# Conv-FFN on one core: seven of twelve units of the first down projection in the seven-product form, parked weight sums every six chunks, and gelu as one ScalarE function

## The chip, the core and the metric

One core of a Trainium2 chip runs one layer of a decoder trunk. TensorE (PE) multiplies, VectorE (DVE) and ScalarE (ACT) prepare operands and evacuate results, GpSimd (POOL) and SyncE (SP) issue most of the DMAs. The metric is the device time of one execution in microseconds (us); the median of several runs is compared.

## What is computed

The layer is an attention mixer and a gated feed-forward block with a short convolution. The change lies in the second:

```python
def conv_ffn(h, w_up, conv_w, conv_b, w_down):
    a, b = jnp.split(h @ w_up, 2, axis=-1)               # h: 256 x 2048, w_up: 2048 x 11264
    ap = jnp.pad(a, ((0, 0), (CONV_WIDTH - 1, 0), (0, 0)))
    c = conv_b
    for j in range(CONV_WIDTH):                          # width 3
        c = c + conv_w[j] * ap[:, j:j + S]
    return (jax.nn.gelu(c, approximate=True) * b) @ w_down   # w_down: 5632 x 2048
...
    h = rms_norm(x, norm_ffn_pre[l])
    y = conv_ffn(h, ffn_w_up[l], ffn_conv_w[l], ffn_conv_b[l], ffn_w_down[l])
    x = x + rms_norm(y, norm_ffn_post[l])
```

All tensors are float32, with 256 tokens, model width 2048 and feed-forward width 5632.

## The kernel before

**Three products for one.** A float32 operand is split into a high and a low part of 128x1024 or 128x512 each. `convert` casts the loaded tile `raw` to `whi` on ScalarE (L163) and subtracts on VectorE (`wlo = raw - whi`, L164). `mm3` (L198 to L200) then multiplies high by high, low by high and high by low. A chunk of weights is one load of 512 KB on SP's queue, one cast, one subtraction and the matmuls that use it. `whi` and `wlo` lie in rings of four buffers: a conversion runs at most some chunks ahead of the matmuls.

**The up part.** Columns of `w_up` are worked in eleven blocks of 512 (c = 0 to 10). A block is 16 chunks, eight for the gate input `a` (accumulators `ua`) and eight for `b` (`ub`). In each chunk of c >= 1 the helper `gemm_cols` runs eight matmuls with the high part, 512 columns wide (L1340), and eight with the low part, 256 wide (L1344); odd chunks take the low part first. After each half `evac` adds two halves of each accumulator into a tile `f` on ScalarE and VectorE (L1361, L1362), and after the block `conv_cols` (L1230 to L1240) does convolution, gelu and gate for four groups of 128 columns: one ScalarE and two VectorE operations for the convolution, then `Square`, a VectorE operation, `Tanh`, a VectorE operation for gelu, then the product with b and a split.

**The first down part.** When c = 5 is done, the 24 finished groups of 128 rows are multiplied with rows 0 to 3071 of `w_down`, in two pairs of column blocks (p = 0, 1, each 1024 columns; `pair_gemm`). A pair is a list of twelve units of two rows of blocks each. A plain unit ("p") is 2 x 4 block products, so 24 matmuls; it converts 2 chunks of 1024 columns. A seven-product unit ("s") replaces the eight block products by seven, 21 matmuls; it needs sums of the activations (`token_sums`, names `sa`, `sm`, `s`) and sums of weight blocks, and converts 3.5 chunks. `PAIR_ORDER` lists the units: six s in each pair before. The four extra accumulators `qd` of the s units lie in the other half of the eight PSUM banks; after the last s unit `end_sums` (L350 to L363) copies and adds them into tiles `ds` (`COPY ds<-qd` on ScalarE, then VectorE adds), which frees those banks for whatever comes next, in pair 1 the accumulators `ua` of block c = 6.

**Parked weight sums.** The sums of weight blocks are made earlier and parked in DRAM (`park_sums`, L235 to L269). One park is: two loads of 512 KB from `w_down` into a staging tile `ta_s` on POOL's queue (L245); two VectorE subtractions and a store of the first half (L257); two more subtractions and a store of the second half (L262). The subtractions are L252, all kept in program order on VectorE. There is a single staging buffer (`STAGE`, tag "sg"), so the loads of a park wait on POOL until the stores of the park before it have landed. `park_a` makes the sums for the first down part; four of them (`EARLY`) are made during the attention, the others in the up part, at steps set by `t0` (a step is one chunk).

**Order.** Each engine runs its own in-order queue. In this region a scheduler decides at build time in which order an engine's instructions stand; at run time an instruction that waits holds up everything behind it on its engine.

Of the kernel before, what the change touches and what calls it, by code (L numbers as in the profile page):

```python
# [37 lines left out]
SC_MLA = (128 + 64) ** -0.5  # L38
GELU_C = math.sqrt(2.0 / math.pi)
GELU_R = math.sqrt(0.044715)  # L40


def trunk_layer(ctx, tc, x, x_cols_in, conv_cols_in, g_mix_post, g_ffn_post, w_in, w_q, w_kv,
# [1116 lines left out]
    def x2_norm(t):  # L1160
        for j in range(4):
            act.activation(jk(f"xj{t}_{j}"), x2[t][j], AF.Square, accum_out=ssh[t][:, j:j + 1])
        v = sb(p3, [P, 1], f"vh{t}")
        vec.tensor_reduce(v, ssh[t], axis=AX.X, op=ALU.add)
        vec.tensor_scalar(v, v, 1.0 / D, EPS, op0=ALU.mult, op1=ALU.add)
        r = rsqrt(v, 1, f"rf{t}", p3)
        r2 = sb(p3, [P, 1], f"rfh{t}")
        vec.tensor_scalar(r2, r, 0.5, None, op0=ALU.mult)
        rf[t] = (r, r2)

# [49 lines left out]
    resid(1)  # L1220
    gT, dsum, dsum_all = [[], []], [], []
    GH, GL = pair_view(gT[0]), pair_view(gT[1])
# [4 lines left out]
    def conv_cols(k, a, b, slot):  # L1227

        w0, w1, w2, cb_ = (cvT[:, 44 * q + k:44 * q + k + 1] for q in range(4))
        cc = sb(p6, [P, 256], f"cc{k}", tag="cc", bufs=3)  # L1230
        uu = sb(p6, [P, 256], f"uu{k}", tag="uu", bufs=3)
        act.activation(cc, a, AF.Identity, scale=w2, bias=cb_)  # L1232
        vec.scalar_tensor_tensor(cc[:, 1:256], a[:, 0:255], w1, cc[:, 1:256], op0=ALU.mult, op1=ALU.add)
        vec.scalar_tensor_tensor(cc[:, 2:256], a[:, 0:254], w0, cc[:, 2:256], op0=ALU.mult, op1=ALU.add)
        act.activation(uu, cc, AF.Square, scale=GELU_R)
        vec.scalar_tensor_tensor(uu, uu, 1.0, cc, op0=ALU.add, op1=ALU.mult)
        act.activation(uu, uu, AF.Tanh, scale=GELU_C)
        vec.scalar_tensor_tensor(uu, uu, 1.0, cc, op0=ALU.add, op1=ALU.mult)
        vec.tensor_tensor(uu, uu, b, op=ALU.mult)  # L1239
        split_to(GH(slot), GL(slot), uu)  # L1240

    def norm_row():
# [3 lines left out]
        for t in range(NT):  # L1246
            vec.tensor_scalar(dg[:, t * P:(t + 1) * P], ident, rf[t][0][:, 0:1], None, op0=ALU.mult)
        pr = pst.tile([P, 512], F32, name="rrow", tag="t")
# [14 lines left out]
    def ffn_up0():  # L1263
# [3 lines left out]
        def evac(acc, q):  # L1267
            f = sb(p6, [P, 1024], f"f{q}_0", tag="f" + "ab"[q], bufs=2)
            for t in range(NT):
                a = f[:, t * 512:(t + 1) * 512]  # L1270
                act.activation(a, acc[t], AF.Copy, scale=rf[t][q][:, 0:1])
                sa[t][q] = a
# [18 lines left out]
        gT[0][:], gT[1][:] = highs(g), lows(g)  # L1291
        dsum_all[:] = [sb(p7, [P, D], f"ds{t}") for t in range(NT)]
        dsum[:] = [[d[:, j * 512:(j + 1) * 512] for j in range(4)] for d in dsum_all]
        norm_row()
# [23 lines left out]
    def sums_tile(name, i):  # L1318
        return sb(*((p3,) if i < 2 else (p6,)), [P, D], f"{name}_{i}", F32R, tag=(f"x2_{i}" if i < 2 else "gp"))

    def x_raws():
        t = sb(p3, [P, D], f"xraw{now[0]}", tag="x2_1")
        more_raw[:] = [raw_of, lambda name: t[:, 0:1024], raw_of, lambda name: t[:, 1024:2048], raw_of, raw_x]

    def g_sums(u):

        if u % 2 == 0:
            s_tiles[u // 2] = sums_tile("s", u // 2)
        hi, lo = (s_tiles[u // 2][:, (u % 2) * 1024 + i * 512:(u % 2) * 1024 + (i + 1) * 512] for i in range(2))
        a, m = (sb(s_pool[0], [P, 512], f"s{n}{u}", tag="hx", bufs=2) for n in "am")  # L1330
# [21 lines left out]
    def ffn_up(c, slot0):  # L1352
# [3 lines left out]
        def evac(acc, q):  # L1356
            f = sb(p6, [P, 1024], f"f{q}_{c}", tag="f" + "ab"[q], bufs=2)
            for i in range(4):
                a = f[:, i * 256:i * 256 + 256]
                sc = (1.0, 0.5)[q]  # L1360
                act.activation(a, acc[i][:, 256:512], AF.Copy, scale=sc)  # L1361
                vec.scalar_tensor_tensor(a, acc[i][:, 0:256], sc, a, op0=ALU.mult, op1=ALU.add)  # L1362
                sa[q].append(a)
# [11 lines left out]
    for i in range(sum(NA) - EARLY):  # L1375
        parked_a.append(park_a(i + EARLY, t0=now[0] + 8 + 15 * i // 2, **STAGE))
    for c in range(1, 6):
# [7 lines left out]
        if c == 5:  # L1385
            at(now[0] + 6, more_raw.clear)
            for u, t in ((2, 8), (3, 11)):
                at(now[0] + t, lambda u=u: g_sums(u))
# [76 lines left out]
    def finish(t, n=4):  # L1465
# [175 lines left out]
```

## Time and profile before

| | |
|---|---|
| median of three runs | 1453.33 us (1453.3 to 1454.87) |
| the profiled execution | 1454.23 us, its span 1452.5 us |
| TensorE clock granted, mean | 0.998 |
| DMA traffic over the span | 359.69 MB, mean 248 GB/s |
| busy in 840 to 860 us (block c = 2) | PE 20.00, VectorE 18.05, ScalarE 12.68 us of 20; DMA share 0.93 |
| busy in 980 to 1000 us (end of c = 5) | PE 20.00, VectorE 12.70, ScalarE 9.95 us of 20; DMA share 0.77 |

The span is the time from the first to the last instruction. A row of a timeline starts with its start and its duration in microseconds, then engine, line, operation, output<-inputs, shape and count; brackets tell how long the engine stood idle before it and what it waited for. Matmuls overlap in the records, so their pitch (from start to start) is what counts, not the duration. In the profiled run block c = 1 of the up part begins at about 772 us, c = 2 at 818.7 us, the two pairs of the first down part fill 997 to 1119 us, and blocks c = 6 to 10 follow.

### The profile page before, as it was taken

The page shows a single profiled execution, that of the slowest core. Times are in us where ns is not written, and L with a number is a line of the kernel's source. Part 1 is how long each engine was busy: PE and PEld are TensorE (multiplying, and loading weights), DVE is VectorE, ACT ScalarE, POOL GpSimd, SP SyncE. Part 2 cuts the span into 40 slices and gives each one's busy share as a digit, 9 for nine tenths or more (in the row PEclk, how much of TensorE's full clock was granted, in tenths as well). Part 3 has the DMA queues.
Part 4 walks back from the last instruction along what each step waited for, and adds up shares of the span by engine and source line. Part 5 has one row for each costly group of instructions (what it writes and reads, how often), then busy time and mean ns, then how long its engine had stood idle before and what let it go on. Part 6 is the DMA issues. An engine that isn't in the chain of part 4 may idle for free.

```text
span 1452.5 us, 21438 instructions
## 1 busy us (share of the span) xinstructions
PE 1442.0 (99%) x7518; PEld 1233.7 (85%) x7518; DVE 1160.4 (80%) x2056; ACT 864.7 (60%) x1422; POOL 118.2 (8%) x222
## 2 busy tenths in 40 slices
PE   9999999999999999999999999999999999999997
PEld 7888888888898888888888888888888888888886
DVE  7788896766878775888789899876777797987798
ACT  7588864544555655546566565655646565555673
POOL 2022110010000001100000111000000101000000
PEclk9999999999999999999999999999999999999999
DMA  8655376699875759965666898866878888789965
GB/s 309 209 171 163 103 261 188 219 327 294 244 220 178 230 164 319 348 232 183 219 205 208 272 331 288 292 206 210 310 276 262 312 276 292 246 265 309 340 219 203
DMA packets 164684, 359.69 MB, mean 248 GB/s; under 512 B 20816, under 2 KB 31952, under 8 KB 164576
## 3 DMA queue, kind: packets, MB, share of 16 engines
q1 hardware_dynamic: 143152, 282.49, 59.8%
q0 software_dynamic: 21280, 75.56, 15.0%
q8 instruction: 59, 0.97, 0.3%
q14 instruction: 49, 0.40, 0.1%
q10 hardware_dynamic: 144, 0.26, 0.1%
HBM read 323.62 MB, written 34.65 MB: 247 GB/s over the span
## 4 chain that ended last, share of the span: by engine, by line
PE 91%; DVE 4%; ACT 2%; DMA 2%; issue 1%; SPq 0%; DVEq 0%; ACTq 0%
PE ub L1340 10%; PE ua L1340 9%; PE accg L200 9%; PE accg L198 9%; PE accg L199 9%; PE ub L1344 5%; PE ua L1344 5%; PE cd L199 2%; PE cd L198 2%; PE cd L200 2%; DVE wlo L164 2%; DMA raw<-in_ffn_w_up_dram 1%; PE cdc L199 1%; PE cdc L198 1%; PE cdc L200 1%
## 5 line engine op out<-in xcount | busy, mean ns | idle before, releaser
L163 ACT CAST whi<-raw 128x1024 fp32r<-128x1024 f32 (+2 forms) x497 | 504.0, 1023 | 373.9 <-PE accg L200 109.1
L164 DVE TENSOR_TENSOR wlo<-raw,whi 128x1024 fp32r<-128x1024 f32 (+2 forms) x497 | 585.0, 1188 | 172.0 <-ACT whi L163 165.6
L198 PE MATMUL accg<-whi,ahl 128*128 128x512 f32 (+1 forms) x416 | 162.5, 391 | 0.0
L200 PE MATMUL accg<-whi,ahl 128*128 128x512 f32 (+1 forms) x416 | 160.7, 386 | 0.0
L199 PE MATMUL accg<-wlo,ahl 128*128 128x512 f32 (+1 forms) x416 | 159.8, 384 | 0.0
L1340 PE MATMUL ub<-ahl,whi 128*128 128x512 f32 x640 | 154.7, 391 | 0.2 <-DVE uu L1239 0.2
L1340 PE MATMUL ua<-ahl,whi 128*128 128x512 f32 x640 | 154.6, 391 | 0.0
L1340 PEld LDWEIGHTS ub<-ahl,whi 128*128 128x128 f32 x640 | 117.5, 188 | 23.1 <-ACT cc L1232 0.5
L1340 PEld LDWEIGHTS ua<-ahl,whi 128*128 128x128 f32 x640 | 117.6, 188 | 22.7
L198 PE MATMUL accg<-whi,bhl 128*128 128x512 f32 x256 | 100.8, 394 | 0.0
L200 PE MATMUL accg<-whi,bhl 128*128 128x512 f32 x256 | 100.0, 391 | 0.0
L199 PE MATMUL accg<-wlo,bhl 128*128 128x512 f32 x256 | 99.9, 390 | 0.0
L200 PEld LDWEIGHTS accg<-whi,ahl 128*128 128x128 f32 x416 | 78.1, 188 | 15.2
L199 PEld LDWEIGHTS accg<-wlo,ahl 128*128 128x128 f32 x416 | 78.3, 188 | 13.0
L198 PEld LDWEIGHTS accg<-whi,ahl 128*128 128x128 f32 x416 | 78.2, 188 | 12.9
L1344 PEld LDWEIGHTS ub<-ahl,wlo 128*128 128x128 f32 x640 | 82.2, 191 | 3.3
L1344 PEld LDWEIGHTS ua<-ahl,wlo 128*128 128x128 f32 x640 | 82.2, 191 | 3.1
L1344 PE MATMUL ua<-ahl,wlo 128*128 128x256 f32 x640 | 83.7, 283 | 0.0
L1344 PE MATMUL ub<-ahl,wlo 128*128 128x256 f32 x640 | 83.3, 283 | 0.0
L200 PEld LDWEIGHTS accg<-whi,bhl 128*128 128x128 f32 x256 | 48.1, 188 | 10.1
L199 PEld LDWEIGHTS accg<-wlo,bhl 128*128 128x128 f32 x256 | 48.1, 188 | 9.6
L198 PEld LDWEIGHTS accg<-whi,bhl 128*128 128x128 f32 x256 | 48.1, 188 | 9.6
(659 smaller groups left out, 2679.7 us busy)
## 6 DMA issues: line engine op xcount, KB each, us to landing
raw<-in_ffn_w_up_dram SPq DMA_DIRECT2D x142, 512.0 KB, 4.9
raw<-in_w_in_dram SPq DMA_DIRECT2D x105, 512.0 KB, 4.6
raw<-in_ffn_w_down_dram SPq DMA_DIRECT2D x66, 512.0 KB, 5.6
xraw<-in_ffn_w_up_dram SPq DMA_DIRECT2D x34, 512.0 KB, 5.2
raw<-in_w_o_swa_dram SPq DMA_DIRECT2D x32, 512.0 KB, 5.3
raw<-in_w_o_mla_dram SPq DMA_DIRECT2D x26, 512.0 KB, 6.9
raw<-in_w_out_dram SPq DMA_DIRECT2D x26, 512.0 KB, 4.6
ta_s<-in_ffn_w_down_dram POOLq DMA_DIRECT2D x24, 512.0 KB, 5.9
```

Source lines behind the costliest of these rows:

```text
L163: act.copy(hi[:, a:b], raw[:, a:b])
L164: vec.tensor_tensor(lo[:, a:b], raw[:, a:b], hi[:, a:b].bitcast(F32), op=ALU.subtract)
L198: pe.matmul(o, ah, bh, start=start, stop=False)
L199: pe.matmul(o, ah, bl, start=False, stop=False)
L200: pe.matmul(o, al, bh, start=False, stop=stop)
L1340: pe.matmul(acc[i], hi[:, c], hn[p][:, j * 512:(j + 1) * 512], start=p + j == 0, stop=stop)
L1344: pe.matmul(acc[i][:, 0:256], lo[:, c], hn[p][:, j * 512:j * 512 + 256], start=False, stop=False)
```

## The change

- `PAIR_ORDER` has seven s units in both pairs instead of six, each in place of a plain unit; the last s unit and the plain unit behind it stay at the end.
- That makes 14 parks instead of 12. Four are still made early; the ten others are made in blocks c = 1 to 4, one every 6 chunks from step 5 on, where there were eight, one every 7.5 chunks from step 8 on.
- The sums of the activations for the seventh unit (u = 6) are made in c = 5. Their tile shares a buffer with the tile `ds0_1`, into which pair 1's `end_sums` copies its first accumulator; the tiles `ds` are now opened where they are first written, one for each token half and pair.
- Gelu is one ScalarE function instead of two ScalarE and two VectorE operations. The factor 0.5 that the old form needed is gone, so `evac` becomes a copy and an add.

```diff
@@ conv_cols
         act.activation(cc, a, AF.Identity, scale=w2, bias=cb_)
...
-        act.activation(uu, cc, AF.Square, scale=GELU_R)
-        vec.scalar_tensor_tensor(uu, uu, 1.0, cc, op0=ALU.add, op1=ALU.mult)
-        act.activation(uu, uu, AF.Tanh, scale=GELU_C)
-        vec.scalar_tensor_tensor(uu, uu, 1.0, cc, op0=ALU.add, op1=ALU.mult)
+        act.activation(uu, cc, AF.Gelu_apprx_tanh)
         vec.tensor_tensor(uu, uu, b, op=ALU.mult)
@@ ffn_up0
-        dsum_all[:] = [sb(p7, [P, D], f"ds{t}") for t in range(NT)]
-        dsum[:] = [[d[:, j * 512:(j + 1) * 512] for j in range(4)] for d in dsum_all]
@@
+    def first_sums_of(p):
+        for t in range(NT):
+            d = sb(s_pool[0], [P, 1024], f"ds{t}_{p}")
+            for j in range(2):
+                dsum[t][2 * p + j] = d[:, j * 512:(j + 1) * 512]
+        return [dsum[t][2 * p + j] for t in range(NT) for j in range(2)]
@@ g_sums
-        if u % 2 == 0:
-            s_tiles[u // 2] = sums_tile("s", u // 2)
-        hi, lo = (s_tiles[u // 2][:, (u % 2) * 1024 + i * 512:(u % 2) * 1024 + (i + 1) * 512] for i in range(2))
+        if u == 6:
+            s = sb(s_pool[0], [P, 1024], f"s{u}", F32R, tag="ds0_1")
+            hi, lo = s[:, 0:512], s[:, 512:1024]
+        else:
...
@@ ffn_up, evac
-                sc = (1.0, 0.5)[q]
-                act.activation(a, acc[i][:, 256:512], AF.Copy, scale=sc)
-                vec.scalar_tensor_tensor(a, acc[i][:, 0:256], sc, a, op0=ALU.mult, op1=ALU.add)
+                act.copy(a, acc[i][:, 256:512])
+                vec.tensor_tensor(a, acc[i][:, 0:256], a, op=ALU.add)
@@
     for i in range(sum(NA) - EARLY):
-        parked_a.append(park_a(i + EARLY, t0=now[0] + 8 + 15 * i // 2, **STAGE))
+        parked_a.append(park_a(i + EARLY, t0=now[0] + 5 + 6 * i, **STAGE))
...
         if c == 5:
             at(now[0] + 6, more_raw.clear)
-            for u, t in ((2, 8), (3, 11)):
+            for u, t in ((6, 4), (2, 8), (3, 11)):
@@
-                      lambda u: s_of[u], p, d, parked=parked_a[NA[0] * p:])
+                      lambda u: s_of[u], p, lambda p=p: first_sums_of(p), parked=parked_a[NA[0] * p:])
@@
-PAIR_ORDER = ("pppspsspsssp", "ppspspsspssp")
+PAIR_ORDER = ("ppsspsspsssp", "ppsspsspsssp")
...
-LINE_Z = 48
+LINE_Z = 64
```

**Where instructions move.** In block c = 2 the rows of VectorE's queue run from the last subtraction of one park to the first of the next (`ta_s` is the staging tile, `wlo` a weight conversion, `f` an evacuation, `cc` the convolution). Before:

```order
L252 TENSOR_TENSOR ta_s<-ta_s 128x512
L164 TENSOR_TENSOR wlo_8733<-raw_8730,whi_8732 128x1024
L164 TENSOR_TENSOR wlo_8757<-xraw_8729,whi_8756 128x1024
L164 TENSOR_TENSOR wlo_8779<-raw_8776,whi_8778 128x1024
L1362 SCALAR_TENSOR_TENSOR f_2_8691<-ua_0_8446,f_2_8691 128x256
L1362 SCALAR_TENSOR_TENSOR f_2_8691<-ua_1_8447,f_2_8691 128x256
L1362 SCALAR_TENSOR_TENSOR f_2_8691<-ua_2_8448,f_2_8691 128x256
L1362 SCALAR_TENSOR_TENSOR f_2_8691<-ua_3_8449,f_2_8691 128x256
L164 TENSOR_TENSOR wlo_8800<-xraw_8729,whi_8799 128x1024
L1233 SCALAR_TENSOR_TENSOR cc_8950<-f_2_8691,cvT,cc_8950 128x255
L164 TENSOR_TENSOR wlo_8822<-raw_8819,whi_8821 128x1024
L1234 SCALAR_TENSOR_TENSOR cc_8950<-f_2_8691,cvT,cc_8950 128x254
```

Five conversions stand here, and a sixth before the next park's first subtraction, seven rows further on. The same place on VectorE of the changed kernel, from the third and last row of subtractions of a park to the next park:

```order
L162 TENSOR_TENSOR wlo_8719<-raw_8716,whi_8718 128x1024
L250 TENSOR_TENSOR ta_s<-ta_s 128x512 x3
L162 TENSOR_TENSOR wlo_8740<-xraw_8715,whi_8739 128x1024
L162 TENSOR_TENSOR wlo_8762<-raw_8759,whi_8761 128x1024
L1363 TENSOR_TENSOR f_2_8674<-ua_0_8438,f_2_8674 128x256
L1363 TENSOR_TENSOR f_2_8674<-ua_1_8439,f_2_8674 128x256
L1363 TENSOR_TENSOR f_2_8674<-ua_2_8440,f_2_8674 128x256
L1363 TENSOR_TENSOR f_2_8674<-ua_3_8441,f_2_8674 128x256
L162 TENSOR_TENSOR wlo_8783<-xraw_8715,whi_8782 128x1024
L1229 SCALAR_TENSOR_TENSOR cc_8933<-f_2_8674,cvT,cc_8933 128x255
L162 TENSOR_TENSOR wlo_8805<-raw_8802,whi_8804 128x1024
L250 TENSOR_TENSOR ta_s<-ta_s 128x512
```

Four conversions stand between the two parks now. Counted over all ten parks of the up part, the distance from the last subtraction of a park to the first of the next is 4, 2, 4, 4, 4, 4, 5, 4 and 4 conversions; before it was 5, 6, 6, 7, 6, 7 and 5.

The second place is the end of pair 1, VectorE's rows of `end_sums` (`qd_3`, `qd_2`, `qd_1` are extra accumulators, `cd_0` a plain one, the last `wlo` rows belong to block c = 6). Before:

```order
L164 TENSOR_TENSOR wlo_11332<-raw_11329,whi_11331 128x1024
L355 TENSOR_TENSOR ds_7772<-ds_7772,qd_3_10887 128x512
L164 TENSOR_TENSOR wlo_11355<-raw_11352,whi_11354 128x1024
L356 TENSOR_TENSOR ds_7773<-ds_7772,qd_2_10886 128x512
L359 TENSOR_TENSOR ds_7773<-ds_7773,qd_1_10885 128x512
L360 TENSOR_TENSOR ds_7772<-ds_7772,qd_1_10885 128x512
L1410 TENSOR_TENSOR ds_7772<-ds_7772,cd_0_10804 128x512
```

And in the changed kernel:

```order
L162 TENSOR_TENSOR wlo_11308<-raw_11305,whi_11307 128x1024
L162 TENSOR_TENSOR wlo_11331<-raw_11328,whi_11330 128x1024
L353 TENSOR_TENSOR ds_1_11240<-ds_1_11240,qd_3_10852 128x512
L162 TENSOR_TENSOR wlo_11358<-raw_11355,whi_11357 128x1024
L354 TENSOR_TENSOR ds_1_11241<-ds_1_11240,qd_2_10851 128x512
L1412 TENSOR_TENSOR ds_1_11240<-ds_1_11240,cd_0_10769 128x512
L357 TENSOR_TENSOR ds_1_11241<-ds_1_11241,qd_1_10850 128x512
L358 TENSOR_TENSOR ds_1_11240<-ds_1_11240,qd_1_10850 128x512
```

The adds stand one conversion of block c = 6 later than before, and the two that free `qd_1` stand behind the add of a plain accumulator. On ScalarE the copy that starts them (`COPY ds<-qd`) stood behind the casts of the pair's last plain unit; in the changed kernel it stands two casts later, here with the last cast of the plain unit, two casts of block c = 6 and the copy:

```order
L161 CAST whi_11265<-raw_11263 128x1024
L161 CAST whi_11307<-raw_11305 128x1024
L161 CAST whi_11330<-raw_11328 128x1024
L352 COPY ds_1_11240<-qd_0_10849 128x512
L161 CAST whi_11357<-raw_11355 128x1024
```

The copy moved behind the casts of the first two chunks of block c = 6. ScalarE's list also has one `ACT_TABLE_LOAD` more, at the first gelu in block c = 1.

More of the change, by code (lines that the diff above doesn't have):

```diff
@@ L38 @@
 SC_MLA = (128 + 64) ** -0.5
-GELU_C = math.sqrt(2.0 / math.pi)
-GELU_R = math.sqrt(0.044715)
 def trunk_layer(ctx, tc, x, x_cols_in, conv_cols_in, g_mix_post, g_ffn_post, w_in, w_q, w_kv,
@@ L1166, in x2_norm @@
         r = rsqrt(v, 1, f"rf{t}", p3)
-        r2 = sb(p3, [P, 1], f"rfh{t}")
-        vec.tensor_scalar(r2, r, 0.5, None, op0=ALU.mult)
-        rf[t] = (r, r2)
+        rf[t] = r
     w_done = [0]
@@ L1220, in trunk_layer @@
     resid(1)
-    gT, dsum, dsum_all = [[], []], [], []
+    gT, dsum = [[], []], [[None] * 4 for t in range(NT)]
     GH, GL = pair_view(gT[0]), pair_view(gT[1])
@@ L1246, in norm_row @@
         for t in range(NT):
-            vec.tensor_scalar(dg[:, t * P:(t + 1) * P], ident, rf[t][0][:, 0:1], None, op0=ALU.mult)
+            vec.tensor_scalar(dg[:, t * P:(t + 1) * P], ident, rf[t][:, 0:1], None, op0=ALU.mult)
         pr = pst.tile([P, 512], F32, name="rrow", tag="t")
@@ L1270, in evac @@
                 a = f[:, t * 512:(t + 1) * 512]
-                act.activation(a, acc[t], AF.Copy, scale=rf[t][q][:, 0:1])
+                act.activation(a, acc[t], AF.Copy, scale=rf[t][:, 0:1])
                 sa[t][q] = a
@@ L1325, in g_sums @@
     def g_sums(u):
-        if u % 2 == 0:
-            s_tiles[u // 2] = sums_tile("s", u // 2)
-        hi, lo = (s_tiles[u // 2][:, (u % 2) * 1024 + i * 512:(u % 2) * 1024 + (i + 1) * 512] for i in range(2))
+        if u == 6:
+            s = sb(s_pool[0], [P, 1024], f"s{u}", F32R, tag="ds0_1")
+            hi, lo = s[:, 0:512], s[:, 512:1024]
+        else:
+            if u % 2 == 0:
+                s_tiles[u // 2] = sums_tile("s", u // 2)
+            hi, lo = (s_tiles[u // 2][:, (u % 2) * 1024 + i * 512:(u % 2) * 1024 + (i + 1) * 512] for i in range(2))
         a, m = (sb(s_pool[0], [P, 512], f"s{n}{u}", tag="hx", bufs=2) for n in "am")
@@ L1405, in trunk_layer, with pair_add @@
     for p in range(2):
-        d = [dsum[t][2 * p + j] for t in range(NT) for j in range(2)]
         c = pair_gemm(f"d{p}", w_down, 0, 1024 * p, PAIR_ORDER[p], lambda k, t: (GH(k)[:, t * P:(t + 1) * P], GL(k)[:, t * P:(t + 1) * P]),
-                      lambda u: s_of[u], p, d, parked=parked_a[NA[0] * p:])
-        for n_, (o, x_) in enumerate(zip(d, c)):
-            at(now[0] + n_, lambda o=o, x_=x_: vec.tensor_tensor(o, o, x_, op=ALU.add))
+                      lambda u: s_of[u], p, lambda p=p: first_sums_of(p), parked=parked_a[NA[0] * p:])
+        def pair_add(i, p, x_):
+            o = dsum[i // 2][2 * p + i % 2]
+            vec.tensor_tensor(o, o, x_, op=ALU.add)
+        for i, x_ in enumerate(c):
+            at(now[0] + i, lambda i=i, p=p, x_=x_: pair_add(i, p, x_))
     more_raw.clear()
@@ L1476, in result @@
             a, b = 512 * j, 512 * j + 512
-            vec.scalar_tensor_tensor(dsum_all[t][:, a:b], dsum_all[t][:, a:b], r[:, 0:1], x2_all[t][:, a:b], op0=ALU.mult, op1=ALU.add)
-            nc.sync.dma_start(out[t * P:(t + 1) * P, a:b], dsum_all[t][:, a:b])
+            vec.scalar_tensor_tensor(dsum[t][j], dsum[t][j], r[:, 0:1], x2_all[t][:, a:b], op0=ALU.mult, op1=ALU.add)
+            nc.sync.dma_start(out[t * P:(t + 1) * P, a:b], dsum[t][j])
         for j in range(n):
```

## Prediction

> **What bounds the kernel now.** I read the page first: the busy times, then the chain that ended last, then TensorE's own waits, then the pitch of its matmuls.
>
> ```profile
> span 1452.5 us, 21438 instructions
> PE 1442.0 (99%) x7518; PEld 1233.7 (85%) x7518; DVE 1160.4 (80%) x2056; ACT 864.7 (60%) x1422; POOL 118.2 (8%) x222
> ...
> PE 91%; DVE 4%; ACT 2%; DMA 2%; issue 1%; SPq 0%; DVEq 0%; ACTq 0%
> ```
>
> TensorE is busy for 99% of the span and makes 91% of the chain. The view of its waits has three rows in all:
>
> ```profile
> PE warm L76 <- DVE ramp L67: 1.1, 1, 1.1
> PE acckv L199 <- DVE wlo L164: 0.4, 1, 0.4
> PE ub L1340 <- DVE uu L1239: 0.2, 1, 0.2
> ```
>
> So between the first product and the tail TensorE stands still for less than 1 us. Whatever shortens its list shortens the kernel by as much; whatever makes it wait is paid in full. That the others keep up is no matter of course: how far they run ahead decides this case. The pitch comes from the first and last of 28 matmuls in a row in pair 0, and the length of a chunk from two rows of the chain that begin two blocks of the up part, sixteen chunks apart (the third row is used below):
>
> ```profile
> 999.79 0.39 PE L199 MATMUL cd<-wlo,bhl 128*128 128x512 f32 x1
> ...
> 1005.91 0.39 PE L199 MATMUL cd<-wlo,bhl 128*128 128x512 f32 x1
> ```
> ```profile
> 818.88 1.81 PE ua L1340 x8
> ...
> 863.41 1.81 PE ua L1340 x8
> ...
> 930.21 1.81 PE ub L1340 x8
> ```
>
> A 512-wide matmul takes 6.12 / 27 = 0.227 us, a chunk of the up part 44.53 / 16 = 2.78 us.
>
> **What the change removes.** Two plain units (24 matmuls each) become seven-product units (21): 6 matmuls less, 6 x 0.227 = **1.4 us**. This is TensorE's time and nothing covers it, so I take all of it. It is less than 0.2% of the time, about what a measurement of this kernel can tell from no change.
>
> The gelu edit takes 88 VectorE and 44 ScalarE operations away, and the evacuation becomes an add of the same shape:
>
> ```profile
> L1236 DVE SCALAR_TENSOR_TENSOR uu<-uu,cc 128x256 f32<-128x256 f32 x44 | 18.0, 418 | 0.6 <-ACT uu L1235 0.5
> L1238 DVE SCALAR_TENSOR_TENSOR uu<-uu,cc 128x256 f32<-128x256 f32 x44 | 18.0, 417 | 0.0
> ...
> L454 ACT ACT_TABLE_LOAD x1 | 1.3, 1283 | 1.2 <-PEq L1613 1.2
> ```
>
> That is 36 us of VectorE's time, all beside TensorE, which waits for VectorE only 0.2 us in that region: worth 0 to 0.2 us, I take 0. The new table load is 1.3 us of ScalarE in block c = 1, where the conversions are about 8 us ahead (below): 0. The sums for the seventh unit add six short rows to VectorE, which by the end of c = 5 is busy for 12.70 of 20 us (the third engine of the row below): 0. In the pairs an s unit converts 3.5 chunks in 21 x 0.227 = 4.8 us; six of them stood there already, three in a row, without a wait of TensorE. Bounds for the new order of units: 0 to 3 us (one unit's room), I take 0.
>
> ```profile
> 980.00:1000.00 20.00, 20.00 (x112) 17.50 (x111) 12.70 (x22) 9.95 (x18) 0.00 (x0) 1.00 0.77 253
> ```
>
> **What the change adds: the chain of parks.** Ten parks in the up part hang together, because there is one staging tile: subtractions on VectorE, second store on POOL, its landing, the loads of the next park, their landing, its subtractions. One link of the chain can be read from POOL and VectorE around 840 us, the only place of the trace where VectorE waits for such a load:
>
> ```profile
> 837.09 0.68 DVE L252 TENSOR_TENSOR ta_s<-ta_s 128x512 f32<-128x512 f32 x1
> ...
> 849.70 0.69 DVE L252 TENSOR_TENSOR ta_s<-ta_s 128x512 f32<-128x512 f32 x1 [0.64 <-DMA ta_s<-in_ffn_w_down_dram]
> ...
> 851.74 0.69 DVE L252 TENSOR_TENSOR ta_s<-ta_s 128x512 f32<-128x512 f32 x1 [1.01 <-DMA ta_s<-in_ffn_w_down_dram]
> ```
> ```profile
> 838.07 0.54 POOL L262 DMA_DIRECT2D ta<-ta_s  x1 [3.47 <-DVE ta_s L252]
> 843.56 1.06 POOL L245 DMA_DIRECT2D ta_s<-in_ffn_w_down_dram  x2 [4.96 <-DMA ta<-ta_s]
> ...
> 894.51 0.55 POOL L262 DMA_DIRECT2D ta<-ta_s  x1 [2.20 <-DVE ta_s L252]
> 902.90 1.06 POOL L245 DMA_DIRECT2D ta_s<-in_ffn_w_down_dram  x2 [7.85 <-DMA ta<-ta_s]
> ```
>
> The last subtraction ends at 837.8, the store is issued at 838.1, the loads at 843.6, and the first half has landed at 849.7: a link of 11.9 us, of which store and landing are 5.5. Elsewhere they were longer (894.5 to 902.9, 8.4 us). Over 780 to 960 us POOL's waits give the landing of the store (sum, times, longest), and the DMA view the load's median:
>
> ```profile
> POOL ta_s L245 <- DMA ta<-ta_s: 23.7, 4, 7.9
> ...
> ta_s<-in_ffn_w_down_dram POOLq DMA_DIRECT2D x14, 512.0 KB, 6.1
> ```
>
> From store to load is thus 23.7 / 4 + 0.5 for the issue = 6.4 us, and a mean link 0.3 + 6.4 + 6.1 = 12.8. I take **12.3**: the one link measured is 11.9, but in seven of the nine later parks the changed order puts the second subtraction close behind the first, where it waits for the second half (2.0 us later, at 851.7).
>
> Between the links stand VectorE's own rows. The pitches come from this stretch:
>
> ```profile
> 887.53 1.22 DVE L164 TENSOR_TENSOR wlo<-xraw,whi 128x1024 fp32r<-128x1024 f32 x1
> 888.66 1.22 DVE L164 TENSOR_TENSOR wlo<-raw,whi 128x1024 fp32r<-128x1024 f32 x1
> 889.80 0.68 DVE L252 TENSOR_TENSOR ta_s<-ta_s 128x512 f32<-128x512 f32 x1
> 890.40 0.48 DVE L1233 SCALAR_TENSOR_TENSOR cc<-f,cvT,cc 128x255 f32<-128x255 f32 x1
> 890.80 0.68 DVE L252 TENSOR_TENSOR ta_s<-ta_s 128x512 f32<-128x512 f32 x1
> ```
>
> A conversion takes 1.13 us, a subtraction 0.60, a small one about 0.35. From first to last subtraction, parks 2 to 10 hold 36 subtractions, 15 conversions, 24 small rows and 6 of the activation sums: 21.6 + 17.0 + 8.4 + 2 = 49 us. Where does the chain begin? Park 1's second pair of subtractions stands behind the first evacuations of c = 1:
>
> ```profile
> 796.42 0.41 DVE L1362 SCALAR_TENSOR_TENSOR f<-ua,f 128x256 f32<-128x256 f32 x1
> ```
>
> Eight more rows make it end near 800. So park 10 ends at 800 + 9 x 12.3 + 49 = **960**. Behind its last subtraction stands the conversion of the fifteenth chunk of c = 4. The second half of c = 4 begins at 930.2 (row above), and this is its seventh chunk, so TensorE begins it at 930.2 + 6 x 2.78 = 946.9. It takes the high part first, 1.8 us, and the conversion takes 1.2, so the subtraction must end by 947.5. The chain is **12.5 us late**, and TensorE waits as long, because the conversions have no more lead than this:
>
> ```profile
> 922.00 1.23 DVE L164 TENSOR_TENSOR wlo<-raw,whi 128x1024 fp32r<-128x1024 f32 x1 [1.21 <-ACT whi L163]
> ```
>
> This converts the last chunk of c = 4's first half, which TensorE begins at 930.2 - 2.8 = 927.4: 4.2 us of lead, after VectorE itself had waited, so the ring of four is full and the lead cannot grow. (Before c = 2 it is larger, which the start at 800 contains.) What is queued behind a late subtraction is every later conversion, and for those TensorE waits. No part of it comes back later, since TensorE has no slack to give. The two bounds: a link of 10.9 or less gives 800 + 98 + 49 = 947, nothing late; a link of 13.4 gives 970, 22 us late. Put as a pitch: a park with its link takes 12.3 + 49 / 9 = 17.7 us; the change grants six chunks, 16.7 us, and less than that after the late start of the first; before it was 7 to 8 chunks, 19 to 22 us.
>
> **The end of pair 1.** The copy of `end_sums` now stands behind two casts of block c = 6, and the freeing of `qd_1` behind one more conversion and one more add:
>
> ```profile
> 1111.67 0.57 ACT L354 COPY ds<-qd 128x512 f32<-128x512 f32 x1
> ...
> 1114.85 1.05 ACT L163 CAST whi<-raw 128x1024 fp32r<-128x1024 f32 x1 [0.37 <-DMA raw<-in_ffn_w_up_dram]
> 1117.71 1.05 ACT L163 CAST whi<-raw 128x1024 fp32r<-128x1024 f32 x1 [1.81 <-DMA raw<-in_ffn_w_up_dram]
> ```
> ```profile
> 1118.71 0.68 DVE L360 TENSOR_TENSOR ds<-ds,qd 128x512 f32<-128x512 f32 x1
> ```
> ```profile
> 1119.35 0.84 PE L1340 MATMUL ua<-ahl,whi 128*128 128x512 f32 x3
> ```
>
> Before, the last add ends at 1119.39, and the second matmul of c = 6 that needs its bank starts at 1119.58: 0.2 us of room. Now the third chunk's cast (1117.71, held by its load) ends at 1118.8, its subtraction at 1119.9, and four adds of 0.6 follow: 1122.4, that is **2.8 us late**. It would be 0 if that load came earlier, 4 if later.
>
> **Sum** against the profiled execution, 1454.2 (span 1452.5 plus 1.7 around it): 1454.2 - 1.4 + 12.5 + 2.8 = 1468.1. That execution lies 0.9 above the median of the runs, so 1467.2; I predict **1467**.
>
> **Rivals.**
> 1. *The links are short* (the other side: not slower). Stores and loads land 1.4 us sooner per link, and the chain keeps pace; the point is a link of 10.9 us. For it speaks that the first loads in c = 1 meet less traffic and that VectorE gets 36 us back; against it that the only link measured is 11.9 and that ten parks bring more traffic than eight. With the end of pair 1 covered too: 1453.3 - 1.4 = 1452. Chance 0.12. [...]
> 2. *Only the end of pair 1 costs*: 1454.7. Chance 0.14.
> 3. *The chain is partly late*, links of 11 to 11.5 us, 1 to 6 us: 1456 to 1459. Chance 0.08.
> 4. *Waits make TensorE slow too.* At the end of the program, where it has nothing to do after 1444.3, its granted clock falls (the windows' row: the busy time and count of five engines, then the clock, the DMA share and GB/s):
>
> ```profile
> 1444.00:1448.00 4.00, 0.29 (x3) 0.09 (x1) 3.49 (x13) 1.08 (x5) 0.00 (x0) 0.92 0.00 0
> 1448.00:1452.50 4.50, 0.00 (x0) 0.00 (x0) 1.14 (x2) 0.00 (x0) 0.00 (x0) 0.50 0.63 233
> ```
>
> 0.92 over 4 us is half speed for 0.64, so the fall came at 1447.4, after 3.1 us of idleness. My waits are some 1 to 3 us each, ten of them, and mostly stay below that. If three or four went over, and each cost 2 us at half speed on top, with links of 13 us: 1480. Chance 0.08. [...]
> 5. *The change does not do what it says*, that is, the six matmuls stay: 1.4 us, too little to be a case of its own; TensorE's rows of the two pairs speak against it.
>
> **How the numbers follow.** The forecast (1459 to 1477) has 0.58, the rivals the rest. The range leaves out rival 4 and some of rival 1: 1452 to 1477. Slower by over 0.2% (above 1456.2) is the forecast, rivals 3 and 4, less a little: 0.73. Within 0.2%: rivals 1 and 2, 0.24. Faster by over 0.2% would need 2.9 us, twice what leaves TensorE's list: 0.03.
>
> **What would show it.** Right: rows of VectorE waiting for the loads of `ta_s` in blocks c = 1 to 4, some ten of 1 to 3 us; TensorE waiting for `wlo` (L162) there, some 12 us in all; a pitch of parks of 17 to 18 us; a wait of `ua` for the adds into `ds_1` at the start of c = 6. Wrong: parks at a pitch of 16.7 us with conversions still 3 to 4 us ahead of TensorE. The number of matmuls and their pitch of 0.227 us should stay as computed in any case.

## The result, and the profile after

| | before | changed |
|---|---|---|
| median of five runs each, side by side | 1454.48 us (1453.3 to 1459.8) | 1471.8 us (1470.96 to 1474.1) |
| ratio, with its 95% interval | | 1.0117 [1.0098, 1.0136] |
| the profiled execution, its span | 1454.23, 1452.5 us | 1474.1, 1472.3 us |
| TensorE clock granted, mean | 0.998 | 0.993 |

The change costs 17 us; about 14 were forecast (1467 against 1453.3). The page of the changed kernel, first the span and the engines, then the chain of work that ended last:

```profile
span 1472.3 us, 21338 instructions
PE 1449.0 (98%) x7512; PEld 1236.6 (84%) x7512; DVE 1142.5 (78%) x1984; ACT 852.4 (58%) x1384; POOL 122.5 (8%) x230
...
PE 28%; DMA 9%; DVE 5%; issue 3%; ACT 1%; POOL 0%; DVEq 0%; POOLq 0%; ACTq 0%; SPq 0%
```

The matmuls are six fewer, and VectorE and ScalarE have less to do, yet the span is 19.8 us longer. The view of TensorE's waits (what waits, for what; sum, times, longest) and VectorE's one row on the staging tile:

```profile
PE ub L1346 <- DVE wlo L162: 6.1, 4, 2.5
PE ua L1346 <- DVE wlo L162: 5.1, 3, 3.9
...
PE ub L1342 <- ACT whi L161: 0.9, 1, 0.9
PE cdb L197 <- DVE wlo L162: 0.8, 1, 0.8
PE ua L1342 <- DVE ds L358: 0.4, 1, 0.4
```
```profile
DVE ta_s L250 <- DMA ta_s<-in_ffn_w_down_dram: 39.7, 14, 7.8
```

TensorE now waits 6.1 + 5.1 + 0.9 = 12.1 us in the up part, nearly all for the low parts that VectorE makes, and VectorE waits 39.7 us for loads of `ta_s`, where before it was 1.7. That is not all that was lost. The windows' row (busy time and count of five engines, then the clock, the DMA share and GB/s) around three of the waits:

```profile
842.00:845.00 3.00, 1.08 (x9) 0.87 (x7) 1.28 (x2) 1.65 (x4) 0.00 (x0) 1.00 0.89 303
845.00:849.00 4.00, 3.40 (x13) 3.12 (x14) 3.93 (x6) 0.00 (x0) 1.08 (x2) 0.57 0.61 217
...
882.00:886.00 4.00, 0.50 (x3) 0.07 (x1) 3.48 (x8) 1.10 (x2) 0.54 (x1) 1.00 0.33 131
886.00:893.00 7.00, 6.27 (x22) 5.50 (x23) 7.00 (x13) 4.54 (x8) 0.55 (x1) 0.51 0.68 222
...
957.00:961.00 4.00, 1.51 (x8) 0.93 (x6) 3.26 (x7) 2.20 (x4) 0.54 (x1) 1.00 0.56 216
961.00:965.00 4.00, 4.00 (x18) 3.75 (x19) 4.00 (x8) 1.77 (x4) 0.54 (x1) 0.57 0.65 176
```

Each pair of rows shows a wait, and behind it a stretch in which TensorE works at a clock near 0.5: 0.43 x 4 + 0.49 x 7 + 0.43 x 4 = 6.9 us of lost work.

Where the 19.8 us arise can be read from the first matmul of pair 0, of the kernel before and of the changed one:

```profile
996.85 0.39 PE L198 MATMUL cd<-whi,bhl 128*128 128x512 f32 x1
```
```profile
1016.57 0.39 PE L196 MATMUL cd<-whi,bhl 128*128 128x512 f32 x1
...
1137.61 0.84 PE L1342 MATMUL ua<-ahl,whi 128*128 128x512 f32 x3
...
1138.82 1.43 PE L1342 MATMUL ua<-ahl,whi 128*128 128x512 f32 x5 [0.37 <-DVE ds L358]
```

All of it, 19.72 us, is there when the pairs begin. The two pairs then take 1137.61 - 1016.57 = 121.04 us; before, up to 1119.35, they took 122.50. The rest is small: 1.5 us more behind the start of c = 6, most of it the wait for `ds` (0.4) and one for a conversion of the second down part (0.8).

### The profile page after: what moved, and what is told of

Read it like the earlier page. It is cut to its first block, busy times and chain, and to the rows that moved or that the text cites. A ratio compares the mean times of both kernels' runs of the same rounds, so it can differ in the third digit from the quotient of the medians.

```text
span 1472.3 us, 21338 instructions
## 1 busy us (share of the span) xinstructions
PE 1449.0 (98%) x7512; PEld 1236.6 (84%) x7512; DVE 1142.5 (78%) x1984; ACT 852.4 (58%) x1384; POOL 122.5 (8%) x230
## 2 busy tenths in 40 slices
DMA packets 166412, 365.45 MB, mean 248 GB/s; under 512 B 21008, under 2 KB 32144, under 8 KB 166304
## 5 line engine op out<-in xcount | busy, mean ns | idle before, releaser
L162 DVE TENSOR_TENSOR wlo<-raw,whi 128x1024 fp32r<-128x1024 f32 (+2 forms) x501 | 588.3, 1186 | 173.9 <-ACT whi L161 167.4
L1346 PE MATMUL ub<-ahl,wlo 128*128 128x256 f32 x640 | 86.4, 288 | 6.1 <-DVE wlo L162 6.1
L250 DVE TENSOR_TENSOR ta_s<-ta_s 128x512 f32<-128x512 f32 x56 | 38.5, 688 | 40.2 <-DMA ta_s<-in_ffn_w_down_dram 39.7
L198 PEld LDWEIGHTS accg<-whi,bhl 128*128 128x128 f32 x256 | 48.1, 188 | 10.0
```

What stands on the lines that cost most here:

```text
L162: vec.tensor_tensor(lo[:, a:b], raw[:, a:b], hi[:, a:b].bitcast(F32), op=ALU.subtract)
L198: pe.matmul(o, al, bh, start=False, stop=stop)
L250: tc.keep_in_program_order(vec.tensor_tensor(o, x, y, op=ALU.subtract))
L1346: pe.matmul(acc[i][:, 0:256], lo[:, c], hn[p][:, j * 512:j * 512 + 256], start=False, stop=False)
```

## The experiments

The theory is the forecast's: ten parks hang together through one staging tile, a park with its link takes about 18 us, the spacing grants 16.7, and the lateness reaches TensorE through the conversions queued behind the late subtractions. Rivals: the seventh units, the gelu or the end of pair 1 cost the time; VectorE has too much work; the DMA traffic is what is late. A question of its own is what the falls of the clock cost. The intervals compare each kernel with the kernel before as measured in the same session; the waits are those of the one profiled execution.

| kernel | time, us | ratio to before [95%] | waits for `wlo`, `whi` in the up part, us |
|---|---|---|---|
| the change, first measurement | 1471.8 | 1.0117 [1.0098, 1.0136] | 12.1 |
| the change, second | 1472.95 | 1.0131 [1.0117, 1.0145] | 12.8 |
| parks every 7.5 chunks, as before | 1453.15 | 0.9994 [0.9985, 1.0003] | 0 |
| every 7 | 1453.39 | 1.0002 [0.9993, 1.0011] | 0 |
| every 6.5 | 1458.82 | 1.0033 [1.0022, 1.0044] | 3.0 |
| every 5 | 1484.11 | 1.0211 [1.0193, 1.0230] | 22.2 |
| six units, eight parks, every 6 | 1473.87 | 1.0148 [1.0133, 1.0164] | 10.3 |
| two staging tiles, every 6 | 1454.5 | 1.0006 [0.9997, 1.0015] | 1.4 |
| gelu edit alone | 1453.48 | 1.0000 [0.9991, 1.0009] | 0 |
| the change with a longer gelu, in the old form | 1477.33 | 1.0163 [1.0149, 1.0177] | 14.7 |
| five waits filled | 1477.22 | 1.0163 [1.0150, 1.0177] | 6.2 |
| two waits filled | 1476.13 | 1.0157 [1.0143, 1.0171] | 11.3 |

**The spacing undone.** One line, which also puts the first park at step 8 instead of 5 (the next kernel keeps step 5):

```diff
-        parked_a.append(park_a(i + EARLY, t0=now[0] + 5 + 6 * i, **STAGE))
+        parked_a.append(park_a(i + EARLY, t0=now[0] + 8 + 15 * i // 2, **STAGE))
```

> The changed kernel with one number undone: its ten parks in the up part stand every seven to eight chunks from step 8 on, as the eight did before; seven units, gelu and the end of pair 1 stay as changed. Between two parks stand 5 to 7 conversions in place of 4. Theory of the chain (the parks are granted 16.7 us and need 18): a pitch of 20.9 us is granted, the chain keeps pace, TensorE's waits for wlo in blocks c = 1 to 5 fall from 12 us to under 1.5 us, its clock stays at 0.99 or more there, and the time is 1452 to 1455 us, the same as the kernel before. Rival (the seventh unit, the sums for it, gelu or the end of pair 1 cost the time, and the spacing is no matter): 1468 to 1472 us.

Measured 1453.15 us: as the kernel before, though units, gelu and the end of pair 1 are the changed ones. Its view of TensorE's waits, whole:

```profile
PE warm L74 <- DVE ramp L65: 1.1, 1, 1.1
PE cdb L197 <- DVE wlo L162: 0.8, 1, 0.8
```

Nothing is left of the waits in the up part. The whole loss depends on the spacing; the rival falls.

**How much spacing is enough.** With `5 + 7 * i`:

> The changed kernel with parks every seven chunks from step 5 on: 19.5 us granted, against the 18.3 us that a park took where the chain ran without slack. Between parks stand 4, 2, 5, 6, 5, 6, 5, 5 and 5 conversions. Theory of the chain: only the first two links, which stand as close as in the changed kernel, may be late, by 1 to 4 us, and the later ones win it back as lead, not as time: 1453 to 1459 us, waits for wlo 0 to 4 us. Rival (the time does not depend on the spacing): 1468 to 1472 us. Rival (a longer pitch costs in proportion, by traffic): half way, about 1462 us.

Measured 1453.39 us, at the low end, and TensorE waits for no conversion in the up part. VectorE's row on the loads is worth reading beside that:

```profile
DVE ta_s L250 <- DMA ta_s<-in_ffn_w_down_dram: 16.7, 8, 5.6
```

VectorE still waits 16.7 us for loads, and TensorE does not notice: those waits end inside the lead of the conversions. An idle row of VectorE is therefore no proof of a loss.

With `5 + 13 * i // 2`:

> The changed kernel with parks every six and a half chunks (six and seven in turn) from step 5 on. It tests the size of the chain's effect. Between five and six chunks the loss up to block c = 5 grew by 11.6 us (31.3 against 19.7 in their traces); at seven and at seven and a half nothing was lost. Nine half chunks give the last park 12.5 us more and put some four or five conversions of 1.13 us more between parks: the lateness falls by about 7.4 us from 17.8, to 10 us, if it still counts in full; the first three parks stand as close as before. Theory of the chain: 1456 to 1465 us. Rival (any spacing above the 16.7 us pitch suffices, the loss is one of two close neighbours in the order): 1452 to 1455 us. Rival (the loss comes whole or not at all): 1470 to 1473 us.

Measured 1458.82 us, inside the theory's range and below its estimate: 5 us over the kernel before, where 10 us of lateness were estimated. No stretch at half clock is left here (the granted clock is 0.999 in the mean). TensorE's row:

```profile
PE ua L1346 <- DVE wlo L162: 3.0, 4, 1.1
```

With `5 + 5 * i`:

> The changed kernel with parks every five chunks from step 5 on: three or four conversions between parks in place of four. Theory of the chain: links do not shorten with the spacing. From the trace of the changed kernel a link from the second store's issue to the next park's first subtraction is 11.7 us on average, nine of them 105.7, VectorE's rows between 58.5 less some nine conversions of 1.13; from 799 the last park ends near 953, and the conversion between its second and third subtraction is needed nine chunks, 25 us, earlier than before. So the lateness grows from 17.8 to 32 to 35 us: 1485 to 1492 us. Rival (lateness follows the number of parks, not their spacing): 1470 to 1474 us. Rival (every fall of the clock costs on top): 1493 to 1505 us.

Measured 1484.11 us, 30 us over the kernel before and 1 below the theory's range; both rivals fall. TensorE waits 22.2 us:

```profile
PE ub L1346 <- DVE wlo L162: 12.3, 5, 5.7
PE ua L1346 <- DVE wlo L162: 9.9, 5, 3.7
```

So 7.5, 7, 6.5, 6 and 5 chunks cost about 0, 0, 5, 18 and 30 us. The loss starts between seven and six and a half chunks: the step to 6.5 costs 5 us, the next half chunk 13, the next whole one 12. That is where the period of the chain lies: a park with its link took 18.3 us in the changed kernel (from the last subtraction of park 1, at 798.09, to that of park 10, at 962.55, over nine), which is 6.6 chunks.

**Fewer parks, same spacing.** Units and parks of before, spacing six:

```diff
-            for u, t in ((6, 4), (2, 8), (3, 11)):
+            for u, t in ((2, 8), (3, 11)):
...
-PAIR_ORDER = ("ppsspsspsssp", "ppsspsspsssp")
+PAIR_ORDER = ("pppspsspsssp", "ppspspsspssp")
```

> The changed kernel with the units of before (six of twelve in seven-product form in each pair, no sums for a seventh), so eight parks in the up part, still every six chunks from step 5 on. Theory of the chain: pitch and lateness of the first eight parks are as in the changed kernel, some 7 to 10 us of waits for wlo with up to three falls of the clock, and 1.4 us more of matmuls: 1462 to 1469 us. Rival (the seventh unit and the end of pair 1 cost the time): 1453 to 1455 us.

Measured 1473.87 us (1471.63 to 1476.83): the rival falls, but my range was too low. By the medians eight parks cost as much as ten; by the traces, in which this kernel is shown at its fastest, TensorE is 17.0 us late when the pairs begin, against 19.7 and 20.8 in the two traces of the changed kernel.

```profile
PE ua L1346 <- DVE wlo L162: 7.4, 4, 3.1
PE ub L1342 <- ACT whi L161: 2.9, 1, 2.9
```

The idle time, 10.3 us, is at the upper end of the 7 to 10 expected. The three falls of the clock that were named came too, 13.7 us at half clock or 6.8 us of lost work; the range had no room for both. And the lateness does not come evenly: of the change's 19.7 us, 13.7 are there by the middle of c = 3, after six of ten parks (its second half begins at 899.19 instead of 885.51).

**A second staging tile.** Spacing six stays; every second park is staged in two tiles that lie idle until the first down part:

```diff
@@ park_sums
+            if halves:
+                st.extend(sb(s_pool[0], [P, 1024], f"{name}s{i}", tag=h) for i, h in enumerate(halves))
...
-        parked_a.append(park_a(i + EARLY, t0=now[0] + 5 + 6 * i, **STAGE))
+        parked_a.append(park_a(i + EARLY, t0=now[0] + 5 + 6 * i, **STAGE, halves=("ds0_0", "ds1_0") if i % 2 else None))
```

> The changed kernel with a second staging tile: every second park in the up part is staged in two tiles of 128x1024 that lie unused until the first down part, so a park's loads no longer wait for the store of the park just before it. Spacing six and seven units stay; between parks stand 3, 1, 4, 4, 4, 4, 5, 4 and 4 conversions. Theory of the chain (one staging tile ties store, load and subtraction into links of 12 us): without the tie VectorE does not wait for the loads (from 40 us of waits to under 6), TensorE's waits for wlo go from 12 us to under 2, and the time is 1452 to 1455 us. Rival (VectorE has too much work, or the DMA traffic of ten parks at this pitch is what delays the weights): the waits stay and the time is 1465 to 1472 us.

Measured 1454.5 us, and VectorE and TensorE wait no more:

```profile
PE ua L1350 <- DVE wlo L162: 1.4, 1, 1.4
...
DVE ta_s L254 <- DMA ta_s<-in_ffn_w_down_dram: 1.2, 1, 1.2
```

The same parks at the same spacing with the same bytes (365.45 MB in both), only not tied to the store before: the loss is gone. Between 800 and 960 us the DMA engines moved 316 GB/s here and 277 in the changed kernel, so they had room. Neither VectorE's work nor the DMA traffic was the limit; the tie through one buffer was. It is not measurably faster than the kernel before all the same, and neither is any other version here: TensorE's list is only 1.4 us shorter.

**Gelu.** The edit alone, in the kernel before:

> The kernel before with the gelu edit alone: one ScalarE function, and the evacuation as a copy and an add; six seven-product units, parks as before. Theory: 36 us of VectorE's time and 44 operations of ScalarE go from beside TensorE, the load of a table is covered: 1453 to 1454.5 us, no difference. Rival (the table load or the longer function delays a conversion): 1455 to 1457 us. Rival (VectorE's time was worth something): 1450 to 1452.5 us.

Measured 1453.48 us, ratio 1.0000: no effect, as the theory said. The reverse puts the old form of gelu into the changed kernel. It is not quite the kernel that its text announces: `evac` stays as changed, and the factor 0.5 is a third VectorE operation in each group (132 VectorE rows more instead of 88).

```diff
-        act.activation(uu, cc, AF.Gelu_apprx_tanh)
+        act.activation(uu, cc, AF.Square, scale=math.sqrt(0.044715))
+        vec.scalar_tensor_tensor(uu, uu, 1.0, cc, op0=ALU.add, op1=ALU.mult)
+        act.activation(uu, uu, AF.Tanh, scale=math.sqrt(2.0 / math.pi))
+        vec.scalar_tensor_tensor(uu, uu, 1.0, cc, op0=ALU.add, op1=ALU.mult)
+        vec.tensor_scalar(uu, uu, 0.5, None, op0=ALU.mult)
```

> The changed kernel with the gelu of before (two ScalarE and two VectorE operations, the evacuation with its factor 0.5), everything else as changed. If VectorE's rows on the chain of parks count, the chain has up to 16 x 2 rows of 0.41 us more, and three conversions stand in other gaps: 1472 to 1482 us. If the chain is made of transfers alone and the rows fit into VectorE's 40 us of waiting: 1470 to 1473 us. Rival (the new gelu itself causes the lateness): 1453 to 1460 us.

Measured 1477.33 us, 4.4 to 5.5 us above the changed kernel (2.4 and 2.8 us in the traces). The first park's second store is issued later, here first in this kernel and then in the changed one:

```profile
803.24 0.54 POOL L260 DMA_DIRECT2D ta<-ta_s  x1 [24.91 <-DVE ta_s L250]
```
```profile
799.07 0.54 POOL L260 DMA_DIRECT2D ta<-ta_s  x1 [20.70 <-DVE ta_s L250]
```

So the chain starts 4.2 us later. From the end of park 1 to the end of park 10 it then takes 163.9 us, no longer than in the two traces of the changed kernel (164.5 and 166.2): the added rows between the parks fit into VectorE's waits. The range of the first branch was met, but through the start of the chain, not through those rows. VectorE's time is worth nothing where the conversions lead, and something where it holds up the start of the chain. The new gelu does not cause the loss; what the old one without the third operation would cost here was not measured.

**What the falls of the clock cost.** Matmuls that count a chunk's high part again are put just ahead of the waiting ones, so that TensorE works where it stood still:

```diff
+    FILL = {(DFF + 1024, 1): 8, (DFF + 1024, 5.5): 8, (1536, 4): 24, (2048, 7): 8, (DFF + 2048, 4): 8}
...
+        def again(hi, p, n):
+            for m in range(n):
+                pe.matmul(acc[m % 4], hi[:, m % 4 * P:(m % 4 + 1) * P], hn[p][:, 0:512], start=False, stop=False)
...
             for f in ((low, high) if p % 2 else (high, low)):
+                if f is low:
+                    again(hi, p, FILL.get((c0, p), 0))
...
+            again(hi, p, FILL.get((c0, p + 0.5), 0))
```

> The changed kernel with 56 matmuls more, put where TensorE waits longest: 8, 8, 24, 8 and 8 products of a chunk's high part are done again just ahead of the matmuls that wait (blocks c = 2, second half, second and seventh chunk; c = 3, first half, fifth chunk; c = 4, first half, last chunk, and second half, fifth chunk). These products are counted twice, so the output is not the reference's. The parks and the conversions keep their order on VectorE but for one conversion. It tells what the falls of the clock cost. In the changed kernel the waits add up to 12 us and the clock is at half for 13.7 us. Both theories: the 56 matmuls, 12.7 us, lie in the waits, and the clock does not fall after them. Theory A, the clock's loss comes on top of the waits: all 6.8 us come back, 1464 to 1466 us. Theory B, the chain of parks alone sets when the late conversions come, so what the clock lost ahead of a later wait only shortened that wait: the 1.7 us after the last wait come back, the rest turns into longer waits, 1469 to 1471.5 us. Rival (VectorE, not the chain, or too little room in the waits): the extra matmuls show, 1475 to 1485 us.

Measured 1477.22 us, outside both theories' ranges. The half-clock loss fell from 6.8 to 3.4 us, so theory A should have seen at least 3 us come back; none did. But no wait remained at the last filled place, so some of the 56 matmuls were paid in full, and that blurs the answer. A second kernel with less, `FILL = {(DFF + 1024, 1): 8, (1536, 4): 14}`, ran beside the changed kernel itself:

> As the kernel that filled the waits, but only at the first two places and with less: 8 products ahead of the second chunk's low part in the second half of block c = 2, and 14 ahead of the fifth chunk's in the first half of c = 3, 22 matmuls or 5.0 us in waits of 2.5 and 3.9 us and in what these grow to; one conversion stands elsewhere on VectorE. These products are counted twice. The falls of the clock at 845 and 886 us should go (5.1 us of loss in the changed kernel). Theory A (the clock's loss comes on top): 1465 to 1468 us. Theory B (the chain sets the time, the clock's loss before a later wait only shortens that wait): 1470 to 1474 us, like the changed kernel, with longer waits later on.

> The changed kernel itself, run beside the two kernels above on the same chip so that they can be compared with it: 1470 to 1474 us. Its waits for wlo in blocks c = 2 to 4 should again be some 12 us, with stretches of 3.4 us at half clock after the waits above 2 us; if the chain depends on how transfers happen to land, single waits may differ by 1 to 3 us and the stretches may number three to five.

The changed kernel again took 1472.95 us. Its rows where c = 2 begins and where the second half of c = 5 begins, and its stretches of half clock:

```profile
818.03 1.30 PE L1342 MATMUL ua<-ahl,whi 128*128 128x512 f32 x5
...
995.34 0.84 PE L1342 MATMUL ub<-ahl,whi 128*128 128x512 f32 x3
```
```profile
863.00:867.00 4.00, 4.00 (x18) 3.34 (x17) 4.00 (x6) 1.35 (x2) 0.00 (x0) 0.57 0.62 211
...
887.00:894.00 7.00, 5.97 (x18) 5.10 (x19) 6.90 (x14) 3.03 (x6) 0.55 (x1) 0.51 0.85 283
...
945.00:949.00 4.00, 3.75 (x14) 3.37 (x15) 3.93 (x10) 0.43 (x2) 0.54 (x1) 0.57 0.94 303
```

And the same of the kernel with two waits filled:

```profile
817.37 0.84 PE L1348 MATMUL ua<-ahl,whi 128*128 128x512 f32 x3
...
994.68 0.62 PE L1348 MATMUL ub<-ahl,whi 128*128 128x512 f32 x2
```
```profile
863.00:867.00 4.00, 3.96 (x13) 3.25 (x14) 3.98 (x5) 4.00 (x5) 0.12 (x1) 0.58 0.37 106
...
924.00:928.00 4.00, 3.48 (x16) 3.04 (x15) 4.00 (x6) 0.00 (x0) 0.54 (x1) 0.57 0.92 285
```

The changed kernel needs 995.34 - 818.03 = 177.31 us for this stretch, with 12.8 us of waits and 6.8 us lost at half clock. The filled one needs 994.68 - 817.37 = 177.31 us, with 11.3 us of waits, 3.4 us lost at half clock and 22 matmuls (5.0 us) more. Both sums are the same, 19.6 and 19.7 us. (The kernel before needs 155.87 us from row to row, so some 1.7 us more in each lie in none of these.) TensorE did 5 us of additional work and got half of its clock loss back, and arrived at the same moment. That two traces agree to 0.01 us is luck: the first measurement of the changed kernel needs 176.43. By theory A the filled kernel would have needed 3.4 us less, 173.9. How the gain was lost can be followed: counted from the start of c = 2, the filled kernel is 2.8 us ahead in the middle of c = 3 (78.34 against 81.18 us), and waits it away by c = 5. The last subtraction of the last park, in the changed kernel and in the filled one:

```profile
964.40 0.69 DVE L250 TENSOR_TENSOR ta_s<-ta_s 128x512 f32<-128x512 f32 x1
```
```profile
963.75 0.69 DVE L250 TENSOR_TENSOR ta_s<-ta_s 128x512 f32<-128x512 f32 x1
```

It starts 146.4 us behind the start of c = 2 in both. The chain took no notice of what TensorE gained, and it sets the moment: theory B. The median, 1476.13 us, is 2 us above B's range. Up to c = 5 the two are equal, so the difference arises behind it: from the start of c = 6 to the end the filled kernel takes 2.7 us more. About 0.7 of that is a longer wait for `ds` (0.9 us against 0.2) and 0.8 are waits for `wlo` in the second down part; the rest stays open.

## Why the prediction was nearly right

**The six matmuls: right.** 122.50 - 121.04 = 1.46 us; forecast were 1.4.

**Gelu, the sums for the seventh unit, the new order in the pairs: right at 0**, by the run with the gelu alone and by the one with the old spacing.

**The chain of parks: right in kind, place and most of its parts.** From the start of a subtraction to the next, measured on VectorE in the changed kernel: nine links of 11.9 us, with 0.8 us more waiting for the second half, 12.7 where 12.3 were taken; 50.0 us of rows between where 49 were counted; start 798.7 instead of 800. The last park ends at 963.2 instead of 960. Of the signs named, VectorE's waits were larger than "some ten of 1 to 3 us": fourteen, 39.7 us in all, the longest 7.8. TensorE's waits, forecast at some 12 us, came to 12.1, but this agreement is luck: the lateness was 18 us by the last wait, and 5.1 us of it were lost at half clock instead of in waits. Store and loads ahead of the last park:

```profile
943.29 0.54 POOL L260 DMA_DIRECT2D ta<-ta_s  x1 [3.60 <-DVE ta_s L250]
949.13 1.06 POOL L243 DMA_DIRECT2D ta_s<-in_ffn_w_down_dram  x2 [5.30 <-DMA ta<-ta_s]
```

The loads issued at 949.13 let the second subtraction start at 957.74 (below), 8.6 us later, where the one link read before had 8.2 (843.56 to 851.74). Rival 1 needed links of 10.9 us and falls.

**Two terms of the lateness were too small: the chain by 3.2 us, as above, and the row at which the lateness was read by 2.2.** That row was wrong in kind: "Behind its last subtraction stands the conversion of the fifteenth chunk of c = 4." TensorE did not wait there, but two chunks earlier. VectorE's timeline at the last park, then the same low parts on TensorE, changed and before:

```profile
955.73 0.69 DVE L250 TENSOR_TENSOR ta_s<-ta_s 128x512 f32<-128x512 f32 x1 [3.21 <-DMA ta_s<-in_ffn_w_down_dram]
957.74 0.69 DVE L250 TENSOR_TENSOR ta_s<-ta_s 128x512 f32<-128x512 f32 x1 [1.32 <-DMA ta_s<-in_ffn_w_down_dram]
958.35 1.41 DVE L1363 TENSOR_TENSOR f<-ua,f 128x256 f32<-128x256 f32 x4
959.68 1.21 DVE L162 TENSOR_TENSOR wlo<-raw,whi 128x1024 fp32r<-128x1024 f32 x1
960.81 0.68 DVE L250 TENSOR_TENSOR ta_s<-ta_s 128x512 f32<-128x512 f32 x1
961.41 1.22 DVE L162 TENSOR_TENSOR wlo<-raw,whi 128x1024 fp32r<-128x1024 f32 x1
962.55 0.68 DVE L250 TENSOR_TENSOR ta_s<-ta_s 128x512 f32<-128x512 f32 x1
```
```profile
960.95 1.41 PE L1346 MATMUL ub<-ahl,wlo 128*128 128x256 f32 x6 [2.49 <-DVE wlo L162]
```
```profile
942.99 2.08 PE L1344 MATMUL ub<-ahl,wlo 128*128 128x256 f32 x16
```

The chain stands still at the first two subtractions, which wait for the loads, and the first conversion behind those is the one that TensorE misses: it ends 2.3 us before the park does, but is needed in time for 942.99, not for 948.7. At that row the forecast's own chain gives 960 - 2.3 - 943.0 = 14.7 us instead of 12.5, and with the 3.2 us by which the chain was longer, 17.9: the measured lateness there is 960.95 - 942.99 = 17.96.

**The clock (rival 4, chance 0.08) came true in part.** It did fall behind waits of 2.5 to 3.9 us, two of them shorter than the 3.1 us that the prediction went by, and TensorE lost 6.9 us to it. The 2 us that the prediction put down for a fall were an estimate that no row of before shows; the three stretches cost 1.7, 3.4 and 1.7 us. But that is not to be added: by the kernel with two waits filled, a loss ahead of a later wait only shortens that wait. What remains is the stretch behind the last wait, 0.43 x 4 = 1.7 us: 17.96 at 960.95, 19.72 at the pairs.

**The end of pair 1: right in kind, too large.** 2.8 us were forecast, 0.4 came (1.0 at most, in the kernel with 6.5 chunks; none with 7.5). The estimate kept the cast of the third chunk where its load held it before, at 1117.71, 1.6 us ahead of the first matmul of c = 6. It now starts earlier:

```profile
1134.06 1.05 ACT L161 CAST whi<-raw 128x1024 fp32r<-128x1024 f32 x1 [1.15 <-DMA raw<-in_ffn_w_up_dram]
```
```profile
1138.09 0.68 DVE L358 TENSOR_TENSOR ds<-ds,qd 128x512 f32<-128x512 f32 x1
```

That is 3.6 us ahead of c = 6 (1137.61), the bound "if that load came earlier" that the prediction named. The last add ends at 1138.8, just behind the moment at which TensorE wants its bank. Why the load comes earlier I did not test.

**The sum again:** -1.5 for the matmuls, 17.96 for the chain, 1.76 for the clock, 1.5 behind the start of c = 6: 19.7 of the 19.8 us between the two profiled spans. The forecast sum was 13.9 us, so 5.9 were missing: the chain was 5.5 us too small, the clock (1.8) and the rest behind c = 6 (1.1) were put at nothing, and the end of pair 1 was 2.4 too large, which hides as much of the other errors. That 1467 came so near is in that part luck.

## What to carry to other kernels

A prefetch through a single buffer has a period: store, landing, load, landing, and the compute that stands between them, here 18.3 us in all. If work is due more often than that, here every 16.7 us, the delay adds up from one item to the next, and it reaches the bound engine through whatever is queued behind the waiting instruction, here the conversion at 959.68 behind subtractions that waited 3.2 and 1.3 us; compare the spacing with that period, and read the lateness at the first row behind the wait that somebody needs, not at the end of the group. A second buffer (1454.5 us), or a spacing longer than the period (1453.4 at seven chunks, or 19.5 us), removed the loss altogether; a shorter list for the bound engine, here by 1.5 us, cannot pay for it. And losses of an engine that is waiting for such a chain do not add up: in the one pair of traces that tested it, only what is lost after the last wait counted.

## What the runs showed of the hardware

TensorE's clock fell at waits shorter than the 3.1 us read from the end of the kernel before. In the changed kernel TensorE waited 2.52 us up to 845.60, 3.89 us up to 886.39 and 2.49 us up to 960.95, and read in windows of 0.1 us the clock went to half at 845.21, 886.17 and 961.26, that is 2.1, 3.7 and 2.8 us after the wait began. Its other waits in blocks c = 1 to 5 that began at full clock, of 0.52 to 0.88 us, brought no fall; nor did those of the kernel with 6.5 chunks in the up part, 1.1 us at most. The length of a single wait does not decide: with the longer gelu the clock fell at 945.86 in a wait of 0.9 us (945.4 to 946.3), and with two waits filled at 924.41 in one of 0.5 us (924.4 to 924.9). What decides was not shown.

The stretches at half clock lasted 3.41, 6.83 and 3.41 us in the changed kernel, and as long in its second measurement (from 863.22, 887.11 and 945.14). Their starts lay 40.96 and 75.09 us apart in the one and 23.89 and 58.03 in the other, which is 12, 22, 7 and 17 times 3.413. What ends them was not shown either.
